# Eight 4 MB loads moved from ScalarE's DMA queue to SyncE's, between the stores, in an attention-score kernel

## The chip, the cores and the metric

The kernel runs on one core of one Trainium2 chip. The metric is the device time of one execution in microseconds (us). For the kernel before, three runs gave 1062.24, 1062.44 and 1063.06 us, with a median of 1062.44. Engines are named as in the profile: PE is TensorE's matmul, PEld its weight load, DVE is VectorE, ACT is ScalarE, POOL is GpSimd and SP is SyncE; a name with a q (SPq, ACTq) is that engine's sequencer, which issues DMAs.

## The reference

```python
# q, k: float32, batch 8, heads 12, sequence 1024, head_dim 64
return np.einsum('bhid,bhjd->bhij', q, k).astype(np.float32)
```

For each of the 96 (batch, head) pairs the kernel multiplies a 1024 x 64 matrix by the transpose of another. A result is 1024 x 1024 in float32, 4 MB. All 96 results are 402.65 MB to be written; both inputs together are 50.33 MB to be read.

## The kernel before, in words

**Blocks.** The 96 heads are worked on in nine blocks of 2, 2, 4, 8, 16, 16, 16, 16 and 16 heads (numbers 0 to 8). While the heads of one block are multiplied, the inputs of the next block are loaded, cast to float16 and transposed. `EARLY = 3` is the last block that is prepared in a way of its own; the blocks of 16 have numbers from 4 on.

**Input side of a block of 16.** The q tensor of a block is one 4 MB load into `x_sb`, and so is its k tensor. There is one `x_sb` for both, so a load must wait until POOL has cast all that was in it before: `load` (line 152) waits for the events in `input_busy`, and line 161 issues the DMA. POOL casts a tensor in four chunks, each of four casts of 32 partitions (line 210), into one of three `half` buffers. DVE transposes a chunk out of its `half` buffer into the float16 operands (line 229). The operands, `qT` and `kT`, exist twice, for the block in work and for the next. The list `TURNS` (line 81) says at which head of the current block the program writes down the transposes of the next block's eight chunks, four of q and four of k; each one is followed by a try to write down further casts (`to_half`, line 375).

**Output side of a head.** PE works in four steps of two tiles (line 311), into one of two halves of the PSUM, ACT copies each step of 128 x 2048 into one of three `o_sb` buffers of 4 MB (line 288), and SP waits for the last copy and issues the 4 MB store (line 301). A buffer is written again when its store has landed.

**Order of the work.** Every engine works through its own list in the order in which the Python program writes it; semaphores tie the lists together. In `block` (line 391), for each head, the loads that fall on it are put on ACT's list, after the copy of the head's step `u = 1` for a block of 16: `next_load(act)` at heads 1 and 7 (q of the next block, then its k). Loads for block 4 are issued in blocks 2 and 3 by the table `LOADS` (line 82). The stores, and the first loads of the kernel, are on SP's list. Each of the two issuing engines has its own DMA queue: in the profile q1 is SP's and q10 is ACT's. Both are worked off by the same 16 DMA engines, each of which moves an equal part of every 4 MB transfer, eight packets of 32 KB.

Of the kernel before, what the change touches and what calls it, by code (L numbers as in the profile page):

```python
# [59 lines left out]
def kernel(  # L60
# [17 lines left out]
    PE_BLOCKS, EARLY = 2, 3  # L78
    NMAX = max(sizes)
    CHUNK, HALVES = 64 * 32, 3  # L80
    TURNS = (3, 4, 5, 6, 10, 11, 12, 13)
    LOADS = {0: {}, 1: {}, 2: {1: 3}, 3: {2: 1}}

    pool = ctx.enter_context(tc.tile_pool(name="sb", bufs=1))
# [19 lines left out]
    sp = Engine(nc, nc.sync, "sp_done")  # L104
# [18 lines left out]
    n, at = S * D // P * 2, 8 * S // 2  # L123
# [207 lines left out]
    at = 0  # L331
# [17 lines left out]
    def next_load(eng):  # L349
        if stream:  # L350
            b, x = stream.pop(0)
            earlier = (b.i, 0) if x else (b.i - 1, 1)
            assert b.i == EARLY or not any((i, c[0]) == earlier for i, c in casts)
            b.load(x, eng)
# [20 lines left out]
    def to_half(last):  # L375
        while casts:
            i, c = casts[0]
            if i > last or (blocks[i], c[0]) in stream:
                return
            if not (rooms if i == PE_BLOCKS else halves).free():  # L380
                return
            done = blocks[i].cast_quads(*c)
            if i == 2:
                early_busy[:] = [done]
            casts.pop(0)

    def transposed(b, s):
        b.transpose_quads(*s)
        to_half(b.i)

    def block(i, heads, regions, w):
        b = blocks[i]
        nxt = blocks[i + 1] if i + 1 < len(blocks) else None
        for n in heads:
            side = {}
            if nxt and nxt.by_pe:
                if n == 1:
                    side = {
                        u: [
                            lambda x=u // 2: nxt.transpose_rows(  # L400
                                x, regions.next(), dve, nc.vector.tensor_copy
                            )
                        ]
                        for u in (1, 3)
                    }
            elif nxt:
                parts = nxt.chunks()
                at = TURNS if i > EARLY else [m * b.N // len(parts) for m in range(len(parts))]
                some = [s for m, s in zip(at, parts) if m == n]
                side = {0: [lambda s=s: transposed(nxt, s) for s in some]}  # L410
            at = LOADS.get(i, {1: 1, 7: 1})
            if n in at:
                side[at[n]] = side.get(at[n], []) + [lambda: next_load(act)]
            b.scores(n, side, regions, w)
            to_half(i + 2 + (n == b.N - 1))

    for b in blocks[:PE_BLOCKS]:
# [6 lines left out]
    for x in range(2):  # L424
        blocks[0].transpose_rows(
            x, quarters.next(), (dve, act)[x], (nc.vector.tensor_copy, nc.scalar.copy)[x]
        )
        to_half(2)
    block(0, [0], quarters, 1)
    halves_ps = Ring([ps_all[:, 2 * S :], ps_all[:, : 2 * S]])  # L430
    halves_ps.busy = [quarters.busy[2] + quarters.busy[3], quarters.busy[0] + quarters.busy[1]]
    block(0, [1], halves_ps, 2)
    for i in range(1, len(blocks)):
        block(i, range(blocks[i].N), halves_ps, 2)
# [31 lines left out]
```

## Time and profile before

| what | value |
|---|---|
| median of three runs | 1062.44 us |
| the profiled execution | 1062.84 us |
| its span, first to last instruction | 1061.0 us |
| PE / ACT / DVE / POOL busy | 66% / 66% / 41% / 33% of the span |
| moved by DMA | 453.21 MB, mean 427 GB/s |
| stores `out_dram<-o_sb`, SP | 96 of 4096 KB, median 21.8 us from issue to landing |
| loads `x_sb<-in_q_dram`, ACT | 5 of 4096 KB, median 24.1 us |
| loads `x_sb<-in_k_dram`, ACT | 5 of 4096 KB, median 24.3 us |
| TensorE clock granted | 1.00 of full speed |

The profiled execution lies 0.40 us above the median of the runs, and 1.84 us of it lie outside the span. The busy share of an engine is its time in instructions; issuing DMAs and waiting do not count. A store's time to landing holds the time in which it stands in its queue behind earlier ones. The chain of waits is read from the end of the kernel back to its start: each piece is the work that released the next.

### The profile page before, as it was taken

Reading aid. Unit: us, or ns where it says so; the run is one execution under the profiler, and the core shown is the slowest. Engines: PE = TensorE matmul, PEld = TensorE weight load, DVE = VectorE, ACT = ScalarE, POOL = GpSimd, SP = SyncE. Lnnn points to the kernel's source line nnn. Section 1 sums busy time; section 2 is a strip of 40 time slices with the busy share of each in tenths; the row PEclk is TensorE's granted clock in tenths of the full one; section 3 lists DMA queues with packets and bytes.
Section 4 is the critical chain, followed back from the end, with each engine's and each line's share of the span. In section 5 each row is a group of like instructions: output and inputs, shape, how many; then the busy total and the mean of one; then the engine's idle time right before and its main releaser. Section 6 shows DMA issues by size and latency. Waiting matters only on the chain.

```text
span 1061.0 us, 3307 instructions
## 1 busy us (share of the span) xinstructions
PE 700.2 (66%) x1568; PEld 127.3 (12%) x800; DVE 431.0 (41%) x55; ACT 697.1 (66%) x386; POOL 354.2 (33%) x206
## 2 busy tenths in 40 slices
PE   6876744957477748567765856775584777778770
PEld 1111100111011101011111101111110111111110
DVE  2995939029193009339003907600761920000000
ACT  4766655857477747567756756775675777777771
POOL 7927465056380028064006509100913700000000
DMA  9999999999999999999999999999999999999997
GB/s 376 434 435 435 434 434 434 416 421 432 431 434 434 435 429 428 426 435 432 432 422 434 435 427 433 433 434 423 433 429 432 435 434 431 434 434 431 432 431 322
DMA packets 17009, 453.21 MB, mean 427 GB/s; under 512 B 1888, under 2 KB 1888, under 8 KB 2912
## 3 DMA queue, kind: packets, MB, share of 16 engines
q1 hardware_dynamic: 14976, 410.00, 89.7%
q10 hardware_dynamic: 2016, 42.99, 9.8%
q8 instruction: 9, 0.15, 0.0%
q14 instruction: 8, 0.07, 0.0%
HBM read 50.33 MB, written 402.65 MB: 427 GB/s over the span
## 4 chain that ended last, share of the span: by engine, by line
DMA 65%; ACT 16%; PE 7%; DVE 5%; POOL 4%; issue 1%; ACTq 0%; SPq 0%
DMA out_dram<-o_sb 60%; ACT o_sb L288 16%; PE ps_all L311 7%; DVE kT L229 4%; POOL half L210 3%; DMA x_sb<-in_k_dram 2%; DMA x_sb<-in_q_dram 2%; DVE qT L229 1%; DMA o_sb<-in_q_dram 0%; PE ps_all L243 0%; POOL qT L181 0%; DVE kT L250 0%; ACT kT L250 0%; ACTq L36 0%; SPq L169 0%
## 5 line engine op out<-in xcount | busy, mean ns | idle before, releaser
L288 ACT COPY o_sb<-ps_all 128x2048 f32<-128x2048 f32 (+1 forms) x384 | 694.8, 1859 | 333.5 <-DMA out_dram<-o_sb 290.2
L311 PE MATMUL ps_all<-kT,qT 64*128 64x512 f16 x1536 | 696.1, 617 | 328.6 <-ACT o_sb L288 312.8
L210 POOL CAST half<-x_sb 32x2048 f16<-32x2048 f32 x176 | 332.3, 1888 | 482.1 <-DMA x_sb<-in_q_dram 302.2
L229 DVE STREAM_TRANSPOSE qT<-half 128x2048 f16<-128x2048 f16 x22 | 202.6, 9478 | 268.1 <-POOL half L210 268.1
L229 DVE STREAM_TRANSPOSE kT<-half 128x2048 f16<-128x2048 f16 x22 | 202.5, 9539 | 137.5 <-POOL half L210 137.5
L308 PEld LDWEIGHTS <-qT 64*128 64x128 f16 x768 | 124.2, 162 | 897.4 <-issue 878.0
L229 DVE STREAM_TRANSPOSE kT<-kT 128x1024 f16<-128x1024 f16 x2 | 9.4, 4870 | 0.0
L229 DVE STREAM_TRANSPOSE qT<-qT 128x1024 f16<-128x1024 f16 x2 | 9.2, 4780 | 0.0
L210 POOL CAST qT<-o_sb 32x1024 f16<-32x1024 f32 x8 | 8.3, 1035 | 1.2 <-DMA o_sb<-in_q_dram 0.8
L210 POOL CAST kT<-o_sb 32x1024 f16<-32x1024 f32 x8 | 8.3, 1035 | 0.5
L250 DVE COPY qT<-ps_all 128x1024 f16<-128x1024 f16 x2 | 2.4, 1224 | 11.1 <-PE ps_all L243 11.1
L288 DVE COPY o_sb<-ps_all 128x1024 f32<-128x1024 f32 x4 | 4.9, 1225 | 4.4 <-PE ps_all L311 4.4
L243 PE MATMUL ps_all<-ident,qT 128*128 128x128 f16 x16 | 2.1, 311 | 6.8 <-POOL qT L181 6.7
L250 ACT COPY kT<-ps_all 128x1024 f16<-128x1024 f16 x1 | 1.0, 1012 | 4.8 <-PE ps_all L243 4.8
L181 POOL CAST qT<-o_sb 128x512 f16<-128x512 f32 x4 | 2.3, 615 | 3.7 <-DMA o_sb<-in_q_dram 3.7
L250 ACT ACT_TABLE_LOAD x1 | 1.3, 1283 | 2.8 <-issue 2.8
L250 DVE COPY kT<-ps_all 128x1024 f16<-128x1024 f16 x1 | 1.2, 1225 | 4.4 <-PE ps_all L243 4.4
L243 PE MATMUL ps_all<-ident,kT 128*128 128x128 f16 x16 | 2.0, 305 | 0.7 <-ACT o_sb L288 0.7
L181 POOL CAST kT<-o_sb 128x512 f16<-128x512 f32 x4 | 2.4, 618 | 0.3 <-DMA o_sb<-in_q_dram 0.3
L243 PEld LDWEIGHTS ps_all<-ident,qT 128*128 128x128 f16 x16 | 1.5, 141 | 7.1 <-POOL qT L181 7.1
L243 PEld LDWEIGHTS ps_all<-ident,kT 128*128 128x128 f16 x16 | 1.5, 136 | 3.3 <-POOL qT L210 1.6
L359 POOL MEMSET ident<- 128x128 f16 x1 | 0.2, 205 | 0.5 <-SPq L98 0.5
(5 smaller groups left out, 0.7 us busy)
## 6 DMA issues: line engine op xcount, KB each, us to landing
out_dram<-o_sb SPq DMA_DIRECT2D x96, 4096.0 KB, 21.8
x_sb<-in_q_dram ACTq DMA_DIRECT2D x5, 4096.0 KB, 24.1
x_sb<-in_k_dram ACTq DMA_DIRECT2D x5, 4096.0 KB, 24.3
x_sb<-in_q_dram SPq DMA_DIRECT2D x1, 2048.0 KB, 14.6
x_sb<-in_k_dram SPq DMA_DIRECT2D x1, 2048.0 KB, 19.5
o_sb<-in_k_dram ACTq DMA_DIRECT2D x4, 256.0 KB, 4.8
o_sb<-in_q_dram SPq DMA_DIRECT2D x4, 256.0 KB, 5.1
o_sb<-in_q_dram SPq DMA_DIRECT2D x1, 1024.0 KB, 8.2
```

Of the source, the lines that this page charges most:

```text
L181: lambda: nc.gpsimd.tensor_copy(out=rows[:, :, h], in_=self.raw[x][:, h * n : (h + 1) * n].rearrange("p (r d) -> p r d", d=D),),
L210: lambda: nc.gpsimd.tensor_copy(out=dst[q0 : q0 + 32].rearrange("p (r d) -> p r d", d=32), in_=raw[32 * b : 32 * b + 32, c * m : (c + 1) * ...
L229: lambda: nc.vector.transpose(out=dst, in_=buf.rearrange("p (r i) -> p r i", i=32)),
L243: lambda: nc.tensor.transpose(t_ps[:, t], rows[:, t], ident),
L250: lambda: copy(out=dst, in_=t_ps.rearrange("c t m -> c m t")), [done]
L288: lambda: (nc.vector.tensor_copy if by_dve else nc.scalar.copy)(out=dst, in_=ps[:, : w * S]),
L308: return nc.tensor.ldweights(stationary, tile_position=(at, 0))
L311: return nc.tensor.add_instruction(mybir.InstMatmult(name=nc.get_next_instruction_name(), ins=[nc.tensor.lower_ap(moving), nc.tensor.lower ...
L359: cleared = gps.run(lambda: nc.gpsimd.memset(ident, 0.0))
```

## The change

From block 4 on, ACT issues no loads. SP issues them instead: the load of the next block's q right after it has issued the store of head 0 of a block, the load of k right after the store of head 7. The entries of `TURNS` are each one higher. The loads in blocks 2 and 3, which bring the inputs of block 4, stay on ACT. Eight loads move, two in each of the blocks 4 to 7; block 8 has no next one.

```diff
-    TURNS = (3, 4, 5, 6, 10, 11, 12, 13)
+    TURNS = (4, 5, 6, 7, 11, 12, 13, 14)
+    BEHIND = (0, 7)
     LOADS = {0: {}, 1: {}, 2: {1: 3}, 3: {2: 1}}
...
-            at = LOADS.get(i, {1: 1, 7: 1})
+            at = LOADS.get(i, {})
             if n in at:
                 side[at[n]] = side.get(at[n], []) + [lambda: next_load(act)]
             b.scores(n, side, regions, w)
+            if i > EARLY and n in BEHIND:
+                next_load(sp)
             to_half(i + 2 + (n == b.N - 1))
```

## The prediction, on record before the changed kernel ran

> **What bounds the kernel now.** I read the page's part 2 (the span in slices) first, then part 3 (the queues), the chain of waits, the waits, and last the trace's records of single DMA packets and of the semaphore increments by which each of the 16 DMA engines reports its share of a store.
>
> ```profile
> DMA  9999999999999999999999999999999999999997
> GB/s 376 434 435 435 434 434 434 416 421 432 431 434 434 435 429 428 426 435 432 432 422 434 435 427 433 433 434 423 433 429 432 435 434 431 434 434 431 432 431 322
> ...
> q1 hardware_dynamic: 14976, 410.00, 89.7%
> q10 hardware_dynamic: 2016, 42.99, 9.8%
> ```
>
> The DMA engines are busy in every slice but the last, and the two queues' shares add up to 99.5% of 16 engines' span. What varies is the rate: 432 to 435 GB/s in most slices, 416 to 429 in those with a load in them. So the kernel is bound by DMA throughout, there is no idle time to fill, and a load can only be made cheaper by making its packets shorter.
>
> The chain of waits shows the same from the side of the buffers. Each piece is start, length, what:
>
> ```profile
> 327.21 1.88 ACT o_sb L288
> ...
> 334.69 21.72 DMA out_dram<-o_sb
> 356.48 1.88 ACT o_sb L288
> ...
> 363.95 31.79 DMA out_dram<-o_sb
> 395.82 1.88 ACT o_sb L288
> ...
> 425.14 1.88 ACT o_sb L288
> ...
> 855.11 1.88 ACT o_sb L288
> ...
> 1030.74 1.88 ACT o_sb L288
> ```
>
> ACT starts to fill a buffer when the buffer's store has landed, fills it in 7.5 us (356.48 to 363.95), and then the buffer stands in the queue behind the two others. One turn of the three buffers is three stores. Without a load it takes (1030.74 - 855.11) / 6 = 29.27 us, so a store's slot is **9.757 us**. With a load in it a turn takes 395.82 - 356.48 = 39.34 us. The difference is the price of that load on the path that sets the end: 10.07 us. The same subtraction from the chain for the other moved loads gives 9.68, 9.65, 9.66, 10.01, 10.26 and 9.70 (where a load touches two turns, their sum less two turns). For the first, whose turn begins outside the steady state, I take landings from the semaphore records: 199.72 to 229.55 us for a load and two stores, so 10.32. **The eight loads cost 79.35 us, on average 9.92, at best 9.65.** The waits confirm who waits: ACT for stores, not ACT for PE.
>
> ```profile
> ACT o_sb L288 <- DMA out_dram<-o_sb: 290.2, 85, 12.0
> ...
> ACT o_sb L288 <- PE ps_all L311: 40.6, 108, 10.4
> ```
>
> The path is that of one DMA engine. By the semaphore records the median engine finishes a store every 9.685 us, but the last one every 9.76 to 9.77, and falls back to 5.13 us behind the median at the end (1059.75 against 1054.62 us). It does not fall back in the last two stores (9.67 us each), during which SP issues nothing more. I read the 0.08 us as a cost of SP's issues, borne by one engine; that is an inference.
>
> **The change, part by part.**
>
> *The turns of the transposes: nothing.* The engines' lists of both kernels, compared with their waits, are the same on PE, DVE and POOL. DVE has only transposes in its list at that time and POOL only casts, so neither sees at which head the program wrote them down. Only ACT's and SP's lists differ.
>
> *ACT loses eight DMA issues,* of 0.334 us each in the row of line 161, 2.7 us in all. ACT is 66% busy and waits 290.2 us for stores: worth nothing.
>
> *SP gains eight issues,* of 0.333 us by its stores' row, each with a wait for POOL's casts. Queued behind it on SP is the next head's store. SP itself waits 986.5 us for ACT, so the issue costs nothing. The wait is over before SP comes to it: count from ACT's start on a block's head 0. The q load now runs behind the stores of that head and its two forerunners, which land at 3 x 9.757 = 29.3 us; it lands at 39 us. POOL casts a tensor in 31.1 us (16 casts, 283.09 to 314.20), so q is cast at 70 us, and SP reaches the k load when head 7 is copied, at 29.3 + 9.8 + 4 x 9.757 + 7.5 = 85.6 us: 15 us of cover. If it were gone, the next store would be issued later, and two more stores in the queue, up to 19 us, would still cover that.
>
> *The loads stand in line with the stores instead of beside them.* Before, the packet records show the engines taking turns between q1 and q10, so that a load lasts 18 to 21 us at half rate and the stores beside it take twice as long. Now a load has the engines to itself for one slot. The same bytes cross the same full engines, so the first-order effect is **zero**. Three buffers still feed the queue: while the load runs, stores of the next two heads are queued behind it, and ACT's next copy waits for the first of them.
>
> *The second order is the load's own price.* It has two terms. The slot: a load issued by SP should cost what a store issued by SP costs, 9.757 us with its issue, at best the 9.65 of the cheapest load now. And slow packets: 32 KB load packets take 1213 ns at best, as a store's do, but in bursts of 1 to 3 us many take 1300 to 2000 ns. The excess over 1213 ns in the moved loads' packets adds up to 0.10 to 0.80 us for each of the 16 engines per load, mean 0.40; on the last engine the load's mean price over its best is 9.92 - 9.65 = 0.27. The trace of before shows no 4 MB load in line on SP's queue. The nearest rows: the first two ACT loads had 0.00 and 0.06 us of excess; the two 2 MB loads at the start, read in line on SP's queue, had a burst at 21 to 23 us, with no store under way, that raises their 256 packets' mean to 648 ns from 612, 256 x 36 / 16 = 0.58 us per engine for 4 MB. So bursts are not a matter of mixing reads and stores. The bounds of this term are 0 and 0.58 us. I take 0.27, from the eight loads themselves.
>
> *Sum:* 8 x (9.757 + 0.27 - 9.92) = **+0.9 us**. On the profiled execution 1062.84 + 0.9 = 1063.7; it lies 0.4 us above the median, so on the runs' scale 1063.3. The bounds: 8 x (9.65 - 9.92) = -2.2 us, and 8 x (9.757 + 0.58 - 9.92) = +3.3 us.
>
> *A later landing.* Counted from ACT's start on head 7, the k load of block 5 was ready for POOL after 24.2 us (258.92 to 283.09); now it is after three store slots and its own, 39.1 us. From there to the end of the last transpose took 44.5 us (283.09 to 327.62), so the operands are ready at 83.6 us. PE first touches them for the next block some 91.5 us after head 7's start (the weight load at 350.41): 8 us of cover remains of 23. Beyond it come ACT's wait of 2.3 us for each buffer and 12 us of stores still queued (two slots of 9.757 less the 7.5 of a fill) before the DMA engines would run dry. So nothing. The Trainium skill, Perfetto Trace Analysis, section "DMA Optimizations", speaks against this part: it advises one issuing engine for inputs and another for outputs "to allow more dynamic spread". This change gives that up; by that rule the kernel loses time where spread is needed, and the trace shows 22 us of cover in its place.
>
> **The rivals.**
>
> *Slower by slow reads.* With all 16 engines reading at once, a burst hits all of them and the last one can't escape it. For it: the burst at 21 to 23 us came in just such a stretch. Against it: q's 2 MB before it read at 612 ns throughout, and 16 engines reading at once are seen without loss in the mixed loads too. Its price is 0.58 us or more a load: 1062.44 + 3.3 = 1065.7 with one burst per load, 8 x 0.58 more, 1070.4, with two. It decides from 0.43 us a load on (8 x (9.757 + 0.43 - 9.92) = 2.1).
>
> *Faster, the loads free of bursts.* A pure read at 1213 ns a packet costs the best price, 9.65, and the end follows the average engine, which loses 0.45 us per load now (the drop from 432.8 GB/s over the eight load windows adds up to 3.6 us). That gives 1062.44 - 3.6 = 1058.8, or 1060.3 if only the last engine's 2.2 us go. For it: the first two loads show reads without excess. Against it: the path is the last engine's, and the startup burst came without mixing.
>
> *Slower by late operands.* If k lands over 22 us later than counted, PE starts the next block late and the DMA engines run dry. Three further slots (29.3 us) would cost about 7 us at each of four block ends: 1090. Nothing in the trace gives that delay.
>
> *The change does nothing it says* holds for the transposes, surely, and changes no time.
>
> **How the numbers follow.** No measurable change, 0.2% or 2.1 us to either side: 50 in 100, at 1063.3 (its own range 1060.5 to 1064.5). Slow reads: 33, of which most between 1064.5 and 1067. Free of bursts: 14, from 1058.8 to 1060.3. Late operands: 3. 0.2% is about what a measurement of this kernel can tell from no change. The range from 1059.5 to 1067 leaves out the lower part of the fast case, two bursts per load and late operands. Faster 0.14, same 0.50, slower 0.36.
>
> **What would show it.** Right: q10 keeps about 9 MB, q1 takes the rest; a turn of three stores with a load in it stays at 39 to 39.6 us; the loads' time to landing grows from 24 to about 31 us; ACT's wait for stores keeps its size and its longest grows to about 12 + 9.8 us; PE does not wait for DVE at the start of blocks 5 to 8. Wrong: slices that fall below 432 GB/s more than before (slow reads), load turns under 39.0 us (free of bursts), or DMA slices under 9 (a dry queue). Also wrong would be a last engine whose lag over the median at the end is far from 5 us: I take its slot as unchanged.

## The result, and the profile after

The changed kernel took 1065.45 us (median of 8 runs, 1064.43 to 1066.18), the kernel before on the same chip 1062.47 us (8 runs, 1061.91 to 1063.55). The ratio is 1.0025, with a 95% interval of [1.0016, 1.0033]: 3.0 us slower. The time lies in the predicted range. The likeliest case, a move within 0.2%, did not come; the time is that of the rival "slower by slow reads", which was put at 1065.7 us. Ratios here and below leave out executions over 1.5% slower than the fastest of the same kernel: one of e9's eleven (2012.64 us) and three of e8's four.

The profiled execution of the changed kernel took 1064.43 us, the fastest of its runs; its span is 1062.6 us. Against the profiled execution before it is 1.59 us longer. What the traces show of the loss is therefore about half of what the medians show.

Part 2 and part 3 of the page after, the slices of the span and the queues:

```profile
DMA  9999999999999999999999999999999999999996
GB/s 375 434 434 434 433 429 434 429 421 430 434 432 434 432 419 431 434 430 434 434 430 414 433 434 432 433 433 422 428 433 434 434 433 434 433 433 433 433 434 300
...
q1 hardware_dynamic: 16128, 443.55, 97.3%
q10 hardware_dynamic: 864, 9.44, 2.1%
```

The loads have left q10, as meant, and the engines are as full as before. Most slices with a load in them still fall, to 414 to 432 GB/s. The last slice moved less: 300 GB/s against 322. At the end of the kernel some engines have nothing left to do while others still store.

The chain of waits after (start, length, what). A turn of three stores without a load, one with, one without, and near the end:

```profile
357.23 1.88 ACT o_sb L289
...
386.27 1.87 ACT o_sb L289
...
393.75 32.60 DMA out_dram<-o_sb
426.43 1.88 ACT o_sb L289
...
433.90 21.49 DMA out_dram<-o_sb
455.47 1.87 ACT o_sb L289
...
1003.06 1.88 ACT o_sb L289
...
1010.54 21.70 DMA out_dram<-o_sb
1032.33 1.87 ACT o_sb L289
```

In this part of the kernel a turn without a load is 386.27 - 357.23 = 29.04 us, a slot of 9.68, not 9.757; near the end it is 1032.33 - 1003.06 = 29.27 again. The turn with a load is 40.16 us, 11.12 more than one without; six other turns with a load take 38.86, 39.65, 39.87, 38.93, 39.61 and 38.94 us. So the load became dearer on the path, and the slot for a time cheaper.

The waits after (us in total, times, longest):

```profile
ACT o_sb L289 <- DMA out_dram<-o_sb: 292.6, 85, 13.3
...
ACT o_sb L289 <- PE ps_all L312: 40.5, 108, 10.4
PEld L309 <- DVE kT L230: 16.0, 2, 11.7
PE ps_all L312 <- DVE kT L230: 13.3, 2, 10.4
```

The loads among the DMA issues, part 6 of the page after, with the median time to landing in the last column:

```profile
x_sb<-in_q_dram SPq DMA_DIRECT2D x4, 4096.0 KB, 31.8
x_sb<-in_k_dram SPq DMA_DIRECT2D x4, 4096.0 KB, 31.0
```

ACT waits for stores as long as before (290.2 us), and PE waits for transposes no longer than before (13.3 us, in two waits). The loads land after 31 to 32 us, as reckoned, and nobody on the path waits for them.

So the loss is in the DMA engines. Each of the 16 reports its share of a transfer when it has landed; the records do not say which engine a report is from, so "the last engine" is whichever reports last. Below, loads are **beside** the stores when they are on ACT's queue, and **in line** when they are on SP's, between the stores. Two numbers from the records serve for all runs. **Excess** is the time of all 32 KB packets over 1213 ns, summed and divided by 16 engines. **Lag** is by how much the last of the 16 engines reports the last store after the median one.

| kernel (one profiled execution each) | loads | excess, us | median engine ends, us | lag, us |
|---|---|---|---|---|
| before | beside | 4.63 | 1054.62 | 5.13 |
| after | in line | 5.13 | 1054.42 | 6.91 |

The median engine ended no later. The last one did: at 1061.33 us instead of 1059.75. Two more are nearly as late (before, the 14th and 15th end at 1055.63 and 1056.88; after, at 1059.27 and 1060.41). Slow packets cost 0.5 us more per engine, and the last engine lost 1.58 us.

### The profile page after: what moved, and what is told of

The parts are those of the page before. It is cut to its first block, busy times and chain, and to the rows that moved or that the text cites. A ratio compares the mean times of both kernels' runs of the same rounds, so it can differ in the third digit from the quotient of the medians.

```text
span 1062.6 us, 3307 instructions
## 1 busy us (share of the span) xinstructions
PE 700.4 (66%) x1568; PEld 127.4 (12%) x800; DVE 430.9 (41%) x55; ACT 697.0 (66%) x386; POOL 354.4 (33%) x206
## 4 chain that ended last, share of the span: by engine, by line
DMA 65%; ACT 16%; PE 7%; DVE 5%; POOL 4%; issue 1%; ACTq 0%; SPq 0%
DMA out_dram<-o_sb 60%; ACT o_sb L289 16%; PE ps_all L312 7%; DVE kT L230 4%; POOL half L211 3%; DMA x_sb<-in_k_dram 2%; DMA x_sb<-in_q_dram 2%; DVE qT L230 1%; DMA o_sb<-in_q_dram 0%; PE ps_all L244 0%; POOL qT L182 0%; DVE kT L251 0%; ACT kT L251 0%; ACTq L36 0%; SPq L170 0%
```

## The experiments

My theory after the trace: the loads in line cost the late engines more, and the turns of the transposes nothing. The first rival: the later turns have a part in it. In the trace after, the loads behind head 0 (q) also looked dearer than those behind head 7 (k), which gave a second question.

**Which part of the change.** Four kernels, each with a part:

```diff
 e1_turns_only (from before)
-    TURNS = (3, 4, 5, 6, 10, 11, 12, 13)
+    TURNS = (4, 5, 6, 7, 11, 12, 13, 14)
 e2_queue_only (from after)
-    TURNS = (4, 5, 6, 7, 11, 12, 13, 14)
+    TURNS = (3, 4, 5, 6, 10, 11, 12, 13)
 e3_q_in_line (from after)
-    BEHIND = (0, 7)
+    BEHIND = (0,)
-            at = LOADS.get(i, {})
+            at = LOADS.get(i, {7: 1})
 e4_k_in_line (from after)
-    BEHIND = (0, 7)
+    BEHIND = (7,)
-            at = LOADS.get(i, {})
+            at = LOADS.get(i, {1: 1})
```

> Only the TURNS line of the change; all loads stay on ScalarE's queue. Theory A (the whole loss comes from the loads in line with the stores, and the turns change no engine's list): 1062.4 us, within 0.1% of the kernel before. Rival B (the later turns cost something, by a later cast or transpose): part of the +3 us shows here, 1063.5 us or more.

> Only the move of the eight loads to SyncE's queue, with the old TURNS. Theory A: as the changed kernel, about 1065.4 us, and the last DMA engine ends 6 to 7.5 us behind the median one (5.1 in the kernel before). Rival B: the loss shrinks, to 1064 us or less.

> The four q loads go behind the store of head 0 on SyncE's queue, the four k loads stay on ScalarE's at head 7. Theory C (in the changed kernel's trace the bursts of slow packets fall in the q loads, 0.68 to 1.1 us for each of the 16 engines against 0.04 to 0.35 in the k loads, so the q loads in line carry the loss): +2.5 to +3 us, 1065 us. Rival D (each load in line costs the same, and the trace shows chance): half the loss, +1.5 us, 1064 us.

> The four k loads go behind the store of head 7 on SyncE's queue, the four q loads stay on ScalarE's at head 1. Theory C: no loss, 1061.5 to 1062.5 us, as k in line meets few bursts and no longer takes turns with the stores. Rival D: half the loss, +1.5 us, 1064 us.

Measured: e1 1062.44 us, ratio 0.9999 [0.9989, 1.0008], lag 5.13. e2 1065.61, 1.0027 [1.0018, 1.0036], lag 7.19. e3 1064.30, 1.0018 [1.0009, 1.0026], lag 6.40. e4 1064.38, 1.0016 [1.0007, 1.0024], lag 6.73. The turns do nothing, from both sides. The move of the loads makes the whole loss. Theory C (the loads behind head 0 carry the loss) fell: four loads in line cost about 2 us, whichever four, a little more than half of eight.

**Queue or moment.** In the changed kernel the loads are also issued a little later or earlier in the head. e9 gives them that moment, on ACT's queue:

```diff
 e9_act_late (from before, with the TURNS of after)
-            at = LOADS.get(i, {1: 1, 7: 1})
+            at = LOADS.get(i, {0: 3, 7: 3})
```

> The loads stay on ScalarE's queue but are issued after head 0 and head 7, when SyncE issues them in the changed kernel. If the queue makes the loss (in line instead of beside): as the kernel before, 1062 to 1063 us, last engine 5 to 5.5 us behind at the end. If the moment makes it: 1065 us.

Measured: 1062.10 us, ratio 0.9996 [0.9987, 1.0005], lag 5.31. So it is the queue: eight 4 MB loads beside the stores are free of the loss, the same loads at the same moment in line are not. The profiled execution of e9 took 1064.42 us, but it had lost 1.9 us against before ahead of the first moved load (head 15's store landed at 201.61 us, against 199.72). From that landing to the end, the last engine takes 860.03, 859.84 and 859.75 us in the profiles with eight loads beside (before, e1, e9), 861.12 and 863.33 with eight in line (after, e2), and 861.85 and 861.73 with four (e3, e4). The excess, counted from the same landing, is 4.44, 4.21 and 4.59 us beside (before, e1, e9) and 4.73, 5.37 and 5.44 in line (after, e2, e5): on average 0.8 us more per engine, while the last engine of the same three ends 2.0 us later. So, averaged over the engines, more slow packets make less than half of the loss; the rest lies in which engines pay.

**Place or tensor.**

```diff
 e5_swapped (from after)
-    flat = [x.rearrange("b h s d -> (b h s) d") for x in (q, k)]
+    flat = [x.rearrange("b h s d -> (b h s) d") for x in (k, q)]
```

> The changed kernel with q and k exchanged where they are read, so that the load behind head 0 brings k and the one behind head 7 brings q; each result comes out transposed. In the changed kernel's trace the loads behind head 0 have 0.68 to 1.1 us of slow packets per engine, those behind head 7 0.04 to 0.35. Place theory: the loads behind head 0 stay the dearer ones. Tensor theory: the dear ones move to head 7. Time by both: as the changed kernel, 1065 to 1066 us.

Measured: 1065.77 us, 1.0024 [1.0015, 1.0033], lag 6.27. The loads behind head 0 had an excess of 1.73, 0.62, 0.73 and 0.32 us, those behind head 7 0.03, 0.44, 0.61 and 0.33. Three of four pairs go with the place and none clearly with the tensor; e3 and e4 say that in time the places do not differ. Why the bursts prefer a place is open.

**What slows the packets.** Two kernels take the neighbours of a load away:

```diff
 e6_drained (from after)
             if i > EARLY and n in BEHIND:
+                sp.wait([(c, c.count) for c in store_landing.values()])
                 next_load(sp)
 e7_no_stores (from after)
+            if 16 < self.first + n < 93:
+                return
             dma = nc.sync.dma_start(
                 out=of[self.first + n]
```

> Ahead of each of the eight loads SyncE waits until every store has landed, so that all 16 DMA engines begin the load together, with no lag between them. Theory E (in line the late engines pay, as they still read when the others already store again): the last engine's load costs no more than the median one's, within 0.2 us, and its lag over the median at the end falls to 3 us or less. Rival F (the slow packets of the last engines are chance, or their own): lag at the end 5 us or more. Time by both some 40 to 80 us above the changed kernel, from eight drained queues of 5 to 10 us.

> The changed kernel without the stores of heads 17 to 92, which are left out, so that the eight loads in line meet no store. If slow packets come from reads that meet stores (also those of engines that are ahead): the excess over 1213 ns is under 0.1 us per engine and load, and the loads land together on all engines within 0.5 us. If reads alone do it: 0.3 to 0.9 us per load, as in the changed kernel. The time falls to where ACT's copies set the pace, 7.5 to 8 us a head, some 900 us.

Measured: e6 1098.51 us with a lag of 0.12 at the end, e7 817.82 us; one execution each. Both times were put too high. The wait of e6 also stands at heads 0 and 7 of block 8, where no load follows, so e6 drains ten times and not eight, and its end comes eight stores after a drain without a load. The loads in part 6 of e6's page:

```profile
x_sb<-in_q_dram SPq DMA_DIRECT2D x4, 4096.0 KB, 14.1
x_sb<-in_k_dram SPq DMA_DIRECT2D x4, 4096.0 KB, 13.3
```

The same of e7's page:

```profile
x_sb<-in_q_dram SPq DMA_DIRECT2D x4, 4096.0 KB, 12.2
x_sb<-in_k_dram SPq DMA_DIRECT2D x4, 4096.0 KB, 12.3
```

Both begin a load with idle engines, and all 16 engines start together. The load with stores queued behind it takes 1 to 2 us longer than the load with none. The packet records say where. In both, the first packet of each engine is slow (15 or 16 packets, 0.6 to 0.8 us of excess). In e6 there is a second burst in all eight loads, 1.0 to 1.35 us per engine: nearly all of its packets begin 4.1 to 3.5 and 2.5 to 1.6 us before the first engine reports, which is where the last two of an engine's eight begin. In e7 there is none, in any of the seven loads that start on idle engines in the stretch without stores, nor in the first (0.04 us), which comes behind head 16's store. So in these two runs reads are slow **at the end of a load, and only where stores follow in the same queue**; reading alone is not slow behind the first packet, also with all 16 engines at it. That was the first branch of e7's expectation; the 0.6 us at the start I had not expected, nor that the first two loads land over 2 us apart on the engines. In the changed kernel's trace, too, most slow packets begin 2.1 us or less before the first engine reports the load, and go on for the late engines up to 3 us after it. But following stores are not enough: two of the changed kernel's eight loads (the k loads issued in blocks 6 and 7) have 0.06 us of excess or less, with stores behind them as the others have.

The prediction knew one such burst, at 21 to 23 us, and called it a stretch with no store under way. It is the end of a load too: the k load lands from 23 us on, and SP had issued the first store behind it, in the same queue, at 18.50 us. So that row did not show bursts without stores.

Theory E (all engines together pay the same, and the lag goes) is not tested by the lag at the end, because the last two drains, without loads, take it away by themselves. The landings of the loads are nearer: in six of e6's eight loads the last engine is 0.2 to 0.7 us behind the median one, but in the other two, the q loads issued in blocks 5 and 7, a single engine is 1.9 and 2.0 us behind.

**The 0.08 us per store.** The prediction read this as a price of SP's issues, borne by one engine. e8 doubles the issues:

```diff
 e8_two_issues (from before)
-            dma = nc.sync.dma_start(
-                out=of[self.first + n].rearrange("(p t) j -> p (t j)", p=P),
-                in_=buf.rearrange("p t j -> p (t j)"),
-            )
-            out_busy.append(store_landing[id(buf)].start(dma))
+            for lo in (0, 64):
+                dma = nc.sync.dma_start(
+                    out=of[self.first + n].rearrange("(p t) j -> p (t j)", p=P)[lo : lo + 64],
+                    in_=buf.rearrange("p t j -> p (t j)")[lo : lo + 64],
+                )
+                landed = store_landing[id(buf)].start(dma)
+            out_busy.append(landed)
```

> The kernel before with each store issued as two of 64 partitions, same packets, twice the issues. If the 0.08 us per head by which one engine falls back is a cost of SyncE's issues, as the prediction read it: 0.16 us per head, last engine 10 to 12 us behind at the end, 1067 to 1069 us. If it has another source: 5 us behind, 1062 to 1063 us.

Measured: 1227.95 us, and the runs spread from 1114 to 1414, so no ratio is to be had. Part 2 of e8's page, GB/s by slice:

```profile
GB/s 353 235 285 381 325 342 316 331 363 366 250 309 349 369 296 311 383 356 372 307 282 336 348 391 386 400 411 410 400 404 428 411 431 434 427 433 434 427 431 325
```

The slices of e8's page show no lack of work: the queues' shares add up to 98.6% of 16 engines' span, and the rate falls to 235 to 400 GB/s for most of the span (the stores' packets take 1432 ns on average, 1215 in the kernel before). But stores of 64 partitions are not slow in themselves. Until the last load has landed, at 995 us, their packets take 1508 ns on average; after it 1218 ns, at 427 to 434 GB/s and 9.73 us a head. What slows them while inputs are still coming in is open.

That last stretch bears on the question. With two issues a head, the engine that falls back most steadily loses 0.10 us a head against those that keep 9.68, and two others lose about 0.05. One engine bearing 0.08 us for each issue would lose 0.16.

e6 does not settle it either. In the four stores that follow its last load's first store, the last engine takes 9.67 to 9.69 us a store and the median one 9.68 to 9.71, as if none fell back. All 16 landings show otherwise: one engine moves from the middle of the pack to its back. In the stores of heads 77 to 80 the second to last engine lands 0.58, 0.64, 0.71 and 0.80 us after the first, in those of heads 45 to 48 0.61, 0.68, 0.76 and 0.83. Only in the stores that follow a drain without a load (heads 81 to 84 and 88 to 95) no engine falls behind the others: all 16 stay within 0.25 us, and each takes 9.73 us a store. What the 0.08 us is stays open; as a price of SP's issues it is neither shown nor ruled out.

**Per change or per byte.** If the price sits at the end of a load, twice as many loads of half the size should cost twice as much:

```diff
 e10_halves_together (from after; load and next_load take a half of the columns)
             if i > EARLY and n in BEHIND:
-                next_load(sp)
+                next_load(sp, 0)
+                next_load(sp, 1)
 e11_halves_apart
             if i > EARLY and n in BEHIND:
-                next_load(sp)
+                next_load(sp, 0)
+            if i > EARLY and n - 1 in BEHIND:
+                next_load(sp, 1)
 e12_beside_apart: the calls of e11 on ACT's queue, after the copy of u = 3
+                        side[3] = side.get(3, []) + [lambda h=h: next_load(act, h)]
```

> The changed kernel with each load in two DMAs of 2 MB (16 KB packets), one right behind the other: as many changes from loads to stores as in the changed kernel. Control for the next run. By the theory that a change from reads to stores in one queue is the price: 1065.5 us, as the changed kernel, at most 0.5 us more for the shorter packets and the added issues.

> The same halves, the second behind the store of the next head (heads 0 and 1, 7 and 8): sixteen changes from reads to stores instead of eight, the same bytes. Price per change: twice the changed kernel's loss, 1068 to 1069 us, and some 9 us of excess in packets. Price per byte read in line: as the control, 1065.5 us.

> The sixteen 2 MB loads of the run before, at the same heads (0 and 1, 7 and 8, after the last copy), but on ScalarE's queue, beside the stores. If the loss needs loads and stores in one queue: no loss, 1062 to 1063 us. If splitting and spreading the loads costs by itself: part of the 6 us shows, 1064.5 us or more.

Measured: e10 1065.49 us, ratio 1.0029 [1.0019, 1.0040]. e11 1069.09, 1.0059 [1.0042, 1.0077]. e12 1067.53, 1.0049 [1.0036, 1.0062]. The six runs of e11 lie in two groups, 1066.51 to 1066.94 and 1071.24 to 1071.91, so its median stands for neither, and its profile is of the lower one. e10 came as the price per change has it, and so did the median of e11, with twice the loss. But e12, the control, fell against me: spread-out halves cost 4.7 us beside the stores too, where four-megabyte loads cost nothing. So the doubling in e11 can't be put down to the changes between loads and stores in one queue. The packets of e11 don't ask for it either: of the halves behind heads 0 and 7, seven of eight have the burst (up to 1.08 us per engine), while those behind heads 1 and 8 have none beyond what every half shows (0.05 to 0.16), though stores follow them in the same queue too. What e10 does add is the place of the burst: where a load has one, it is in the second half (0.60 to 0.88 us behind head 0, up to 0.33 behind head 7), not in the first (0.04 to 0.15). Why sixteen spread loads cost more on either queue is open. In e12 the slow packets are those of the stores (excess of the 32 KB packets, nearly all of them stores here, 6.18 us in all; 4.63 before, loads included), while its load packets are fast.

## Why the prediction was right, and which step was off

- **What bounds the kernel.** Right for every kernel here that writes all results: the engines stay full, and the time goes with the end of the last engine. Over the profiles with the eight loads in line (after, e2, e5, and e10 with its halves together) the median engine ends at 1055.2 us on average and the lag is 7.3; with them beside (before, e1, e9) 1055.0 and 5.2. These profiles end 2.3 us apart, and 2.1 of it is lag.
- **The turns of the transposes: nothing.** Right: e1 0.9999, and e2 as the whole change.
- **ACT's and SP's issues: nothing.** Right as to the time. SP's eight load issues took 0.81 to 1.21 us instead of 0.333, each following a store's issue at once; nobody waited.
- **SP's wait for the casts, and the later landing: covered.** Right: 31 to 32 us to landing, no new wait on PE. What was off is a detail, ACT's longest wait for a store: put at 12 + 9.8 us, it is 13.3. The load's slot adds to the usual wait of 2.3 us, not to the 12 that a load beside had made already.
- **The load's price, the step that was off in size.** Taken as 9.757 + 0.27 = 10.03 us per load on the path, with a bound of 0.58 for the second term. From one landing to the next on the last engine, the loads of the changed kernel took 11.60, 9.82, 11.05, 10.55, 10.82, 9.88, 10.35 and 9.67 us, on average 10.47: 0.71 over the slot, above the bound. The median engine took 10.01. e2 and e5 give 10.38 and 10.56 on the last, 9.83 and 10.07 on the median. The 0.27 was read from loads beside stores, where the last engine paid less than the median one (by landings 9.88 against 10.16, slots taken off); in line it pays more. The row that was nearer, the reads in line at the start with 0.58 us, stood in the prediction as the bound, and I took the other. That row was also misread as a burst with no mixing of reads and stores: a store was queued behind the load (issued at 18.50 us).
- **The slot taken as unchanged: wrong, in the other direction.** In the profiled execution after, other engines are last for some 41 stores, and they have a slot of 9.68. The account: 8 x (10.47 - 9.92) = +4.4; 41 x (9.757 - 9.68) = -3.2; 0.5 us already lost ahead of block 4 (200.21 against 199.72 us), which the change cannot have made; together +1.7, measured +1.59. With the median run 3.0 us slower, other executions may get less of that back; no trace shows it. So two signs read ahead of time failed: no turn with a load lies between 39 and 39.6 us (three are under 39.0, on the cheaper slot, four over 39.6), and the lag is 6.91 us, not 5. Whether the 0.08 us of the dearer slot are a price of SP's issues stays open.
- **Partly luck.** The sum gave +0.9 us and the medians +3.0. With the load's measured price and the slot kept, as the prediction has it, the sum would have been +4.4 us, outside its own bounds of -2.2 to +3.3 and only just inside the range. In the profiled execution two terms were off in opposite directions; that the time came so near to the rival's 1065.7 is not to its credit.
- **Why the late engines pay more in line** is argued (they still read when the others store again), agrees with six of e6's eight loads and not with the other two, and is not shown.
- **The rivals.** "Slower by slow reads" came true in its time, 1065.7 against 1065.45. Slow reads do come, at the end of loads in line, with about 0.5 us of excess per load in the changed kernel. But its mechanism was wrong in two points. It is not that all 16 engines read at once, for e7 reads at full speed behind the first packet; there stores must follow. And a burst does not cost all engines the same: over a load in line the median engine takes 10.01 us and the last 10.47, and the excess per engine explains less than half of what the last engine lost. "Free of bursts" and "late operands" did not come. The Trainium skill's advice of one issuing engine for inputs and another for outputs (Perfetto Trace Analysis, "DMA Optimizations") held in its result, 0.25% here, though no wait for spread was the reason.

No run that writes all results beats the kernel before: e1 and e9 equal it, all others are slower. e7 is faster because it leaves out 76 stores.

## What to carry to other kernels

With all DMA engines full, moving these transfers to another queue changed nothing to first order, and what was left was decided by the last of the 16 engines: read the landings, not only the mean rate, and read all 16 of them, because an engine that falls back can stay unseen inside the pack for several stores. Large loads fared better in a queue of their own beside the stores than in line with them, by 0.25% for eight loads; and fewer, larger loads fared better than many spread ones in either queue. Where a small term has two rows to be read from, take the row with the same neighbours in the queue.

## What the runs showed of the hardware that I had not expected

- Reads just ahead of stores in the same queue: the last two 32 KB packets of a load are slow on all engines, 1.0 to 1.35 us together (e6), and not without stores behind (e7). In the changed kernel and in e11 some loads with stores behind them have no such burst.
- The first read packet after idle engines: 0.6 to 0.8 us of excess on each engine (e6, e7).
- Stores in two DMAs of 64 partitions: 1114 to 1414 us instead of 1062, packets of 1432 ns instead of 1215, but 1218 ns once the last load had landed (e8).
- One of 16 equally loaded engines ends 5 us after the median, 0.08 us a store (before). After a drain with a load behind it one engine still falls back; after a drain without one none does in eight stores, at 9.73 us a store for all (e6).
- Sixteen spread 2 MB loads cost about 0.5%, in line or beside (e11, e12), where eight 4 MB loads beside cost nothing (e1, e9).
